# S5 set-up on VectorE, a new order of layer 0's input rows, and a norm shift subtracted last, in a two-layer encoder trunk

## The chip, the cores and the metric

The kernel runs on one core of a Trainium2 chip. The metric is the device time of one execution in microseconds (us), the median of the runs. TensorE (PE) multiplies matrices, and PEld is its loading of weights. VectorE (DVE), ScalarE (ACT) and GpSimd (POOL) work on elements, and SyncE (SP) issues the loads.

## What is computed

256 frames and 16 meta tokens (272 columns) of width 2048 pass through two layers, in float32. Each layer is a mixer and a SwiGLU feed-forward block, and each of them is wrapped in a residual and a norm, `x <- LayerNorm(alpha * x + f(x))`. Layer 0's mixer is one input projection whose 15 blocks of 128 rows go to two parts: rows 0 to 7 to S5, a complex diagonal state space (eight quarters q of 128 channels here), rows 8 to 14 to latent attention (8 to 11 the query latents, 12 and 13 the key and value latents, 14 the rotary key). For S5 the reference has:

```python
dt = jnp.exp(log_dt)[:, None]
mag = jnp.exp(dt * a_re)
ab_re = mag * jnp.cos(dt * a_im)
ab_im = mag * jnp.sin(dt * a_im)
...
bb_re = f_re[..., None] * b_re - f_im[..., None] * b_im
...
_, _, s_re, s_im = lax.associative_scan(...)   # s_t = ab * s_(t-1) + bb u_t, complex
y = (einsum('lbgp,gjp->blgj', s_re, c_re) - einsum('lbgp,gjp->blgj', s_im, c_im))
```

Layer 1's mixer is Mamba-2; it is not touched.

## The kernel before

**Matmuls.** `linear()` (L131) walks through a projection in the order of the table SEQ (L58), block by block of 128x128. `weights()` (L113) brings eight blocks at a time: SP loads a tile `st` of 128x1024 (four buffers), ACT casts it to `hi` (L126), DVE computes `lo = st - hi` (L127; three buffers each). Every block takes three matmuls: hi by the high part of the input (L173), hi by its low part (L174), lo by its high part (L175). A tile thus feeds 24 matmuls, and PE can go on only when ACT and DVE have done their parts. Accumulators `mm_...` have three PSUM buffers, which an evacuation frees.

**Order.** The program is written in plain loops, and a scheduler of the tile framework sorts each engine's instructions; then every engine runs its own in that order, and an instruction that waits holds up all behind it on its engine. The order at the places of the change is shown below for that reason.

**Layer 0's mixer** (L516). in0b is the first projection, rows 0, 1 and 8, all three together while the input is loaded and split (L536, L537: `xin`, `h`); then in0a, rows 9 to 14 one by one; then uq and ukv, which need the norms of the latents (`rms`, L561), the values, and the scores of 8 heads with rows 2 to 7 between them. `evac_u` (L591) receives rows 0 and 1: on row 0 it calls `S.load()`, loads the constants, and calls `S.setup()` and `S.run(0)`.

**S5** (L972). `load` brings the parameters `prm`. `setup` (L1034) computes on DVE the two exponentials (`expm1`), on ACT the sine and cosine, and then powers of the complex numbers with `cmul` (L985), six operations for one product, on POOL: `pr, pi` (powers of the step), `wr, wi` (repeated squares), and from them the tables `er, ei, gr, gi`. `prep(q)` (L1140) builds the matrices `gb` and `ca` of a quarter on POOL (`pp`), which ACT copies; `prep_pe(q)` (L1173) transposes gb on PE (`gt_p`), multiplies (`kb_p`), and makes the rotation tables `ec, es` on DVE from er, ei, gr, gi. `run(q)` (L1208) writes u to DRAM and loads it shifted (`u2`), multiplies (`w_p`), rotates and scans on DVE, and forms the output (`s5y_p`); then it prepares the next quarter.

**The norms.** `ln_add` (L303) adds a row of a projection's result to x as it comes out of PSUM (L311). The sums that the norm needs are taken of `x - k`, with k a shift that is known only after row 0 (`ln_sums`, L319, copied at L328); so each of the rows 1 to 15 has k subtracted first (L308), and its addends are added then. Four norms go this way: behind out0a, dn_b0, out1c and dn_b1.

## Time and profile before

| | |
|---|---|
| median of 3 runs | 2692.54 us (2691.0 to 2699.14) |
| the profiled execution | 2692.83 us, its span 2691.0 us |
| busy share of the span | PE 98%, PEld 92%, DVE 65%, ACT 49%, POOL 12% |
| DMA | 173 GB/s in the mean |
| granted TensorE clock, mean of the span | 0.99 of full speed (2.4 GHz); the other level is 0.50 (1.2 GHz) |

The page gives busy times over the whole execution; what an engine waited for, and when, is read from the lists of waits, from windows, and from the timelines of single engines. Times in them are us from the start of the span. Lines are those of the kernel before.

### The profile page before, as it was taken

What the parts mean: (1) busy time and instruction counts of PE and PEld (TensorE: products, weight loads), DVE (VectorE), ACT (ScalarE), POOL (GpSimd) and SP (SyncE); (2) the same over time, 40 slices, a digit from 0 to 9 for tenths busy, and PEclk for the clock granted to TensorE, in tenths of its full rate; (3) what the DMA queues carried; (4) which work ended last, traced back from release to release, by engine and by line L of the source; (5) the groups of instructions that cost most, each with busy time, mean ns of one, the idle gap of its engine ahead of it and who ended that gap; (6) DMA issues with size and microseconds to landing.
All of it is one profiled execution on the core that took longest, in us unless ns stands there. A gap on an engine that the chain in (4) does not pass through costs nothing.

```text
span 2691.0 us, 48314 instructions
## 1 busy us (share of the span) xinstructions
PE 2634.4 (98%) x19344; PEld 2468.3 (92%) x19344; DVE 1737.1 (65%) x2944; ACT 1316.6 (49%) x2168; POOL 331.2 (12%) x484
## 2 busy tenths in 40 slices
PE   9899999999999999999999999999999999999997
PEld 9677999999999999999999899999998888888886
DVE  7768678444444445669778875788975555555565
ACT  5545447334334334448656653554664443444443
POOL 5844040000000000210002110111300000000022
PEclk9898999999999999999999999999999999999998
DMA  7233544555555554545645555544555555555553
GB/s 246 85 111 90 194 151 166 177 173 175 178 173 175 177 173 165 184 165 173 220 156 195 176 175 186 177 168 149 181 196 188 188 188 187 187 188 188 183 189 116
DMA packets 139666, 465.01 MB, mean 173 GB/s; under 512 B 14832, under 2 KB 30000, under 8 KB 139312
## 3 DMA queue, kind: packets, MB, share of 16 engines
q1 hardware_dynamic: 139296, 461.71, 51.5%
q8 instruction: 151, 2.47, 0.4%
q14 instruction: 75, 0.61, 0.1%
q10 hardware_dynamic: 144, 0.21, 0.0%
HBM read 458.58 MB, written 3.28 MB: 172 GB/s over the span
## 4 chain that ended last, share of the span: by engine, by line
PE 88%; DVE 6%; POOL 3%; ACT 1%; issue 1%; DMA 0%; SPq 0%; DVEq 0%; ACTq 0%; POOLq 0%
PE mm_gu_b L170 6%; PE mm_gu_a L170 5%; PE mm_in L170 4%; PE mm_gu_a L175 4%; PE mm_gu_a L173 4%; PE mm_gu_a L174 4%; PE mm_gu_b L175 3%; PE mm_gu_b L173 3%; PE mm_gu_b L174 3%; PE mm_gu_b L171 3%; PE mm_dn_b L170 3%; PE mm_dn_a L170 3%; PE mm_in L174 2%; PE mm_gu_a L171 2%; PE mm_in L173 2%; PE mm_in L175 2%
## 5 line engine op out<-in xcount | busy, mean ns | idle before, releaser
L127 DVE TENSOR_TENSOR lo_gu_b<-st_gu_b,hi_gu_b 128x1024 fp32r<-128x1024 f32 x176 | 215.6, 1225 | 228.7 <-ACT hi_gu_b L126 228.7
L127 DVE TENSOR_TENSOR lo_gu_a<-st_gu_a,hi_gu_a 128x1024 fp32r<-128x1024 f32 x176 | 216.0, 1227 | 176.7 <-ACT hi_gu_a L126 176.1
L126 ACT CAST hi_gu_b<-st_gu_b 128x1024 fp32r<-128x1024 f32 x176 | 184.8, 1050 | 290.4 <-issue 155.7
L126 ACT CAST hi_gu_a<-st_gu_a 128x1024 fp32r<-128x1024 f32 x176 | 184.7, 1049 | 232.7 <-issue 121.1
L339 POOL TENSOR_TENSOR ln_s<-ln_s,ln_q 128x272 f32<-128x272 f32 (+1 forms) x58 | 71.9, 1239 | 1563.2 <-ACT ln_q L334 1562.8
L170 PE MATMUL mm_gu_b<-m,hi_gu_b 128*128 128x512 f32 x704 | 246.8, 395 | 0.0
L127 DVE TENSOR_TENSOR lo_in<-st_in,hi_in 128x512 fp32r<-128x512 f32 (+1 forms) x268 | 184.9, 723 | 82.1 <-ACT hi_in L126 78.3
L126 ACT CAST hi_in<-st_in 128x512 fp32r<-128x512 f32 (+1 forms) x268 | 158.4, 636 | 116.9 <-PE mm_in L174 38.1
L175 PE MATMUL mm_gu_a<-mix,lo_gu_a 128*128 128x272 f32 (+1 forms) x704 | 203.4, 289 | 1.7 <-DVE lo_gu_a L127 1.6
L174 PE MATMUL mm_gu_a<-mix,hi_gu_a 128*128 128x272 f32 (+1 forms) x704 | 203.5, 289 | 0.0
L175 PE MATMUL mm_gu_b<-mix,lo_gu_b 128*128 128x272 f32 x704 | 203.2, 289 | 0.0
L174 PE MATMUL mm_gu_b<-mix,hi_gu_b 128*128 128x272 f32 x704 | 202.7, 288 | 0.0
L173 PE MATMUL mm_gu_a<-mix,hi_gu_a 128*128 128x272 f32 (+1 forms) x704 | 202.5, 288 | 0.0
L173 PE MATMUL mm_gu_b<-mix,hi_gu_b 128*128 128x272 f32 x704 | 202.5, 288 | 0.0
L171 PE MATMUL mm_gu_b<-m,lo_gu_b 128*128 128x256 f32 x704 | 197.2, 280 | 0.0
L170 PE MATMUL mm_gu_a<-m,hi_gu_a 128*128 128x512 f32 x544 | 190.7, 395 | 0.0
L170 PE MATMUL mm_in<-f,hi_in 128*128 128x512 f32 x512 | 181.0, 396 | 0.0
L127 DVE TENSOR_TENSOR lo_dn_a<-st_dn_a,hi_dn_a 128x1024 fp32r<-128x1024 f32 x88 | 107.8, 1225 | 110.4 <-ACT hi_dn_a L126 110.0
L126 ACT CAST hi_dn_a<-st_dn_a 128x1024 fp32r<-128x1024 f32 x88 | 92.3, 1049 | 162.2 <-PE mm_dn_a L174 78.6
L170 PEld LDWEIGHTS mm_gu_b<-m,hi_gu_b 128*128 128x128 f32 x704 | 132.5, 188 | 31.2
L127 DVE TENSOR_TENSOR lo_dn_b<-st_dn_b,hi_dn_b 128x1024 fp32r<-128x1024 f32 x88 | 107.6, 1224 | 78.0 <-ACT hi_dn_b L126 77.6
L126 ACT CAST hi_dn_b<-st_dn_b 128x1024 fp32r<-128x1024 f32 x88 | 92.3, 1049 | 129.8 <-PE mm_dn_b L170 46.9
(549 smaller groups left out, 8630.0 us busy)
## 6 DMA issues: line engine op xcount, KB each, us to landing
st_gu_a<-in_w_gu_a SPq DMA_DIRECT2D x176, 512.0 KB, 3.9
st_gu_b<-in_w_gu_b SPq DMA_DIRECT2D x176, 512.0 KB, 4.2
st_in<-in_w_in SPq DMA_DIRECT2D x140, 512.0 KB, 3.4
st_dn_a<-in_w_dn_a SPq DMA_DIRECT2D x88, 512.0 KB, 4.2
st_dn_b<-in_w_dn_b SPq DMA_DIRECT2D x88, 512.0 KB, 3.8
st_in1h<-in_w_in1h SPq DMA_DIRECT2D x34, 512.0 KB, 3.3
st_out1a<-in_w_out1a SPq DMA_DIRECT2D x32, 512.0 KB, 3.3
st_out0b<-in_w_out0b SPq DMA_DIRECT2D x16, 512.0 KB, 3.5
```

Of the source, the lines that this page charges most:

```text
L126: nc.scalar.copy(hi[:, j:j + w], st[:, j:j + w])
L127: nc.vector.tensor_tensor(lo[:, j:j + w], st[:, j:j + w], hi[:, j:j + w], op=ALU.subtract)
L170: nc.tensor.matmul(ps[m].rearrange("p (a b) -> p a b", a=2), lhsT=wh, rhs=x2, start=st, stop=False)
L171: nc.tensor.matmul(o, lhsT=wl, rhs=xh, start=False, stop=left[m] == 0)
L173: nc.tensor.matmul(o, lhsT=wh, rhs=xh, start=st, stop=False)
L174: nc.tensor.matmul(o, lhsT=wh, rhs=xl, start=False, stop=False)
L175: nc.tensor.matmul(o, lhsT=wl, rhs=xh, start=False, stop=left[m] == 0)
L339: nc.gpsimd.tensor_tensor(st["s2"], st["s2"], q, op=ALU.add)
```

## The change

The complex numbers of S5's set-up are packed, real and imaginary part side by side in one tile (`z1`, `pw`, `wz`, `ez`, `gz`), and their 18 products go from POOL's `cmul` to DVE: ten squares in three instructions (`zsqr`) and eight products in four (`zmul`). POOL loses 108 instructions. in0b takes rows 8, 9 and 10, in0a rows 11 to 14 and then 0 and 1. `S.load()` comes first of all, the constants and `S.setup()` behind in0b; `S.run(0)` is called behind uq and `S.run(1)` behind the values, and the first `prep_pe(0)` and `prep(1)` move from the set-up into `run(0)`. In `ln_add` the subtraction of k comes behind the addends.

```diff
@@ -56,8 +56,8 @@
 
 
 SEQ = {
-    "in0a": seq_rows([9, 10, 11, 12, 13, 14], range(16)),
-    "in0b": seq_rows([0, 1, 8], range(16), 3),
+    "in0a": seq_rows([11, 12, 13, 14, 0, 1], range(16)),
+    "in0b": seq_rows([8, 9, 10], range(16), 3),
     "in0_2": seq_rows([2], range(16)),
     "in0_3": seq_rows([3], range(16)),
     "in0_4": seq_rows([4], range(16)),
@@ -304,11 +304,11 @@
 
         nc, pool, n, xs = self.nc, st["pool"], st["n"], st["xs"]
         x = xs[i]
-        if i:
-            nc.vector.tensor_tensor(x, x, st["k"], op=ALU.subtract)
         for a in (p, q):
             if a is not None:
                 nc.vector.tensor_tensor(x, x, a, op=ALU.add)
+        if i:
+            nc.vector.tensor_tensor(x, x, st["k"], op=ALU.subtract)
         self.ln_sums(st, i, x)
         if st["hx"] is not None:
             if i >= st["late"]:
@@ -589,20 +589,21 @@
             S = S5(self, s5, ps, u)
 
             def evac_u(m, p):
-                if m == 8:
+                nc.scalar.copy(u[:, m, :], p)
+                S.run(m)
+
+            def evac_0(m, p):
+                if m < 8:
+                    nc.scalar.copy(u[:, m, :], p)
+                else:
                     evac_a(m, p)
-                    return
-                nc.scalar.copy(u[:, m, :], p)
-                if m == 0:
-                    S.load()
-                    for t, a in ((self.ident, "ident"), (self.vecs, "vecs"), (cos, "cos"), (sin, "sin"),
-                                 (perm, "perm")):
-                        nc.sync.dma_start(t, A[a])
-                    S.setup()
-                S.run(m)
-
-            self.linear("in0b", rhs, evac_u, N)
-            self.linear("in0a", rhs, evac_a, N)
+
+            S.load()
+            self.linear("in0b", rhs, evac_0, N)
+            for t, a in ((self.ident, "ident"), (self.vecs, "vecs"), (cos, "cos"), (sin, "sin"), (perm, "perm")):
+                nc.sync.dma_start(t, A[a])
+            S.setup()
+            self.linear("in0a", rhs, evac_0, N)
 
             qk = self.res.tile([P, DT, N], F32, tag="x", name="qk")
             qr = pool.tile([P, 4, N], F32, tag="qr", name="qrope")
@@ -618,6 +619,7 @@
             def evac_k(m, p):
                 nc.scalar.copy(qk[:, 8 + m, :], p)
 
+            S.run(0)
             self.linear("ukv", lambda k, m: kn[:, :, k, :], evac_k, N)
 
 
@@ -640,6 +642,7 @@
             self.dump("kr", kr)
             self.dump("v", v)
 
+            S.run(1)
             probs = self.scores(pool, work, pa, 0, qk, qr, kr)
             for h in range(8):
                 nxt = self.scores(pool, work, pa, h + 1, qk, qr, kr) if h < 7 else None
@@ -1004,6 +1007,29 @@
         eng.tensor_tensor(t1, ai, br, op=ALU.mult)
         eng.tensor_tensor(oim, t3, t1, op=ALU.add)
 
+    def zmul(self, o, a, b, shape):
+
+        v = self.nc.vector
+        n = 2 * int(np.prod(shape))
+        t1, t2 = (self.t(f"zm{c}", [n], tag=f"cm{c}", bufs=1) for c in range(2))
+        if len(shape) == 2:
+            t1, t2 = (x.rearrange("p (r a b) -> p r a b", r=2, b=shape[1]) for x in (t1, t2))
+            br, bi = (b[:, c].unsqueeze(2).unsqueeze(1).to_broadcast([P, 2] + shape) for c in range(2))
+        else:
+            t1, t2 = (x.rearrange("p (r a) -> p r a", r=2) for x in (t1, t2))
+            br, bi = (b[:, c].unsqueeze(1).to_broadcast([P, 2] + shape) for c in range(2))
+        v.tensor_tensor(t1, a, br, op=ALU.mult)
+        v.tensor_tensor(t2, a, bi, op=ALU.mult)
+        v.tensor_tensor(o[:, 0], t1[:, 0], t2[:, 1], op=ALU.subtract)
+        v.tensor_tensor(o[:, 1], t1[:, 1], t2[:, 0], op=ALU.add)
+
+    def zsqr(self, o, a):
+        v = self.nc.vector
+        t = self.t("zs", [64], tag="cm2", bufs=1).rearrange("p (r a) -> p r a", r=2)
+        v.tensor_tensor(t, a, a, op=ALU.mult)
+        v.scalar_tensor_tensor(o[:, 1], a[:, 0], 2.0, a[:, 1], op0=ALU.mult, op1=ALU.mult)
+        v.tensor_tensor(o[:, 0], t[:, 0], t[:, 1], op=ALU.subtract)
+
     def expm1(self, x, name):
 
         v = self.nc.vector
@@ -1048,7 +1074,9 @@
         v.scalar_tensor_tensor(r, k, -1.9350051879882812e-3, r, op0=ALU.mult, op1=ALU.add)
         v.scalar_tensor_tensor(r, k, -3.0199159819e-7, r, op0=ALU.mult, op1=ALU.add)
         v.tensor_scalar(r, r, -3.1415925, 3.1415925, op0=ALU.max, op1=ALU.min)
-        sn, cs, hs, ab = (self.t(n_, [32], tag=t_) for n_, t_ in (("sn", "sn"), ("csn", "csn"), ("hs", "pp2"), ("ab", "ro3")))
+        z1 = self.t("z1", [2, 32])
+        cs, sn = z1[:, 0], z1[:, 1]
+        hs, ab = (self.t(n_, [32], tag=t_) for n_, t_ in (("hs", "pp2"), ("ab", "ro3")))
         nc.scalar.activation(ab, r, AF.Abs)
         nc.scalar.activation(sn, r, AF.Sin)
         nc.scalar.activation(cs, ab, AF.Sin, bias=T.halfpi, scale=-1.0)
@@ -1059,22 +1087,17 @@
         v.tensor_tensor(q2, cs, cs, op=ALU.mult)
         v.tensor_tensor(q, q, q2, op=ALU.add)
         v.tensor_scalar(q, q, -0.5, 1.5, op0=ALU.mult, op1=ALU.add)
-        v.tensor_tensor(sn, sn, q, op=ALU.mult)
-        v.tensor_tensor(cs, cs, q, op=ALU.mult)
-
-        pr, pi = self.t("pr", [32, 5]), self.t("pi", [32, 5])
+        v.tensor_tensor(z1, z1, q.unsqueeze(1).to_broadcast([P, 2, 32]), op=ALU.mult)
+
+        pw = self.t("pw", [2, 5, 32])
+        pr, pi = pw[:, 0].rearrange("p k s -> p s k"), pw[:, 1].rearrange("p k s -> p s k")
         self.pr, self.pi = pr, pi
-        nc.gpsimd.memset(pr[:, :, 4], 1.0)
-        nc.gpsimd.memset(pi[:, :, 4], 0.0)
-        v.tensor_tensor(pr[:, :, 3], mag, cs, op=ALU.mult)
-        v.tensor_tensor(pi[:, :, 3], mag, sn, op=ALU.mult)
-
-        def pw(o, a, b):
-            self.cmul(nc.gpsimd, pr[:, :, o], pi[:, :, o], pr[:, :, a], pi[:, :, a], pr[:, :, b], pi[:, :, b], [32])
-
-        pw(2, 3, 3)
-        pw(1, 2, 3)
-        pw(0, 2, 2)
+        nc.gpsimd.memset(pw[:, 0, 4], 1.0)
+        nc.gpsimd.memset(pw[:, 1, 4], 0.0)
+        v.tensor_tensor(pw[:, :, 3], z1, mag.unsqueeze(1).to_broadcast([P, 2, 32]), op=ALU.mult)
+        self.zsqr(pw[:, :, 2], pw[:, :, 3])
+        self.zmul(pw[:, :, 1], pw[:, :, 2], pw[:, :, 3], [32])
+        self.zsqr(pw[:, :, 0], pw[:, :, 2])
         self.m4 = self.t("m4", [32])
         v.tensor_tensor(q, mag, mag, op=ALU.mult)
         v.tensor_tensor(self.m4, q, q, op=ALU.mult)
@@ -1098,27 +1121,21 @@
         v.tensor_tensor(fi, fi, den, op=ALU.mult)
         self.fr, self.fi = fr, fi
 
-        er, ei = self.t("er", [32, 8]), self.t("ei", [32, 8])
-        gr, gi = self.t("gr", [32, 9]), self.t("gi", [32, 9])
-        wr, wi = self.t("wr", [32, 7], tag="pp0"), self.t("wi", [32, 7], tag="pp1")
-
-        def sqr(o, i):
-            self.cmul(nc.gpsimd, wr[:, :, o], wi[:, :, o], wr[:, :, i], wi[:, :, i], wr[:, :, i], wi[:, :, i], [32])
-
-
-        self.cmul(nc.gpsimd, wr[:, :, 1], wi[:, :, 1], cs, sn, cs, sn, [32])
-        self.cmul(nc.gpsimd, wr[:, :, 0], wi[:, :, 0], wr[:, :, 1], wi[:, :, 1], wr[:, :, 1], wi[:, :, 1], [32])
+        ez, gz = self.t("ez", [2, 32, 8]), self.t("gz", [2, 32, 9])
+        er, ei, gr, gi = ez[:, 0], ez[:, 1], gz[:, 0], gz[:, 1]
+
+        wz = self.t("wz", [2, 7, 32], tag="u2", bufs=1)
+        self.zsqr(wz[:, :, 1], z1)
+        self.zsqr(wz[:, :, 0], wz[:, :, 1])
         for j in range(1, 7):
-            sqr(j, j - 1)
-        for (tr, ti, lo, n) in ((er, ei, 0, 8), (gr, gi, 3, 9)):
-            nc.gpsimd.memset(tr[:, :, 0], 1.0)
-            nc.gpsimd.memset(ti[:, :, 0], 0.0)
+            self.zsqr(wz[:, :, j], wz[:, :, j - 1])
+        for (tz, lo, n) in ((ez, 0, 8), (gz, 3, 9)):
+            nc.gpsimd.memset(tz[:, 0, :, 0], 1.0)
+            nc.gpsimd.memset(tz[:, 1, :, 0], 0.0)
             w, j = 1, lo
             while w < n:
                 m = min(w, n - w)
-                br = wr[:, :, j:j + 1].to_broadcast([P, 32, m])
-                bi = wi[:, :, j:j + 1].to_broadcast([P, 32, m])
-                self.cmul(nc.gpsimd, tr[:, :, w:w + m], ti[:, :, w:w + m], tr[:, :, 0:m], ti[:, :, 0:m], br, bi, [32, m])
+                self.zmul(tz[:, :, :, w:w + m], tz[:, :, :, 0:m], wz[:, :, j], [32, m])
                 w, j = 2 * w, j + 1
         self.er, self.ei, self.gr, self.gi = er, ei, gr, gi
 
@@ -1134,8 +1151,6 @@
             self.zb.append((gb, ca, kb, m4))
         self.ready = {}
         self.prep(0)
-        self.prep_pe(0)
-        self.prep(1)
 
     def prep(self, q):
 
@@ -1208,6 +1223,9 @@
     def run(self, q):
         nc, T, u = self.nc, self.T, self.u
         v = nc.vector
+        if q == 0:
+            self.prep_pe(0)
+            self.prep(1)
         gb, ca, kb, m4 = self.zb[q % 2]
         gt, ec, es = self.ready.pop(q)
```

The order of the instructions, at three places. **DVE at the start of the program**, before (`h` is the low part of the input, `lo_in0b` the low part of a weight tile):

```order
L127 TENSOR_TENSOR lo_in0b_107<-st_in0b_104,hi_in0b_106 128x1024
L208 TENSOR_TENSOR h_82<-xin,h_82 128x2x272 x2
L127 TENSOR_TENSOR lo_in0b_147<-st_in0b_144,hi_in0b_146 128x1024
L208 TENSOR_TENSOR h_82<-xin,h_82 128x2x272
L127 TENSOR_TENSOR lo_in0b_180<-st_in0b_177,hi_in0b_179 128x1024
L208 TENSOR_TENSOR h_82<-xin,h_82 128x2x272
L127 TENSOR_TENSOR lo_in0b_213<-st_in0b_210,hi_in0b_212 128x1024
```

and with the change:

```order
L1039 TENSOR_SCALAR ex_328<-prm 128x32
L1040 TENSOR_SCALAR ex_323<-prm 128x32
L1110 TENSOR_TENSOR den<-prm 128x32
L1041 TENSOR_SCALAR ex_324<-ex_323 128x32
L1042 TENSOR_SCALAR ex_324<-ex_324 128x32
L1043 SCALAR_TENSOR_TENSOR ex_325<-ex_324,ex_323 128x32
L1049 TENSOR_SCALAR ex_i<-ex_324 128x32
L1044 SCALAR_TENSOR_TENSOR ex_325<-ex_324,ex_325 128x32
L1050 TENSOR_TENSOR ex_327<-ex_i,ex_328 128x32
L1045 TENSOR_SCALAR ex_326<-ex_325 128x32
L1047 SCALAR_TENSOR_TENSOR ex_326<-ex_326,ex_325 128x32 x5
L127 TENSOR_TENSOR lo_in0b_109<-st_in0b_106,hi_in0b_108 128x1024
```

Fifteen operations on the S5 parameters (`prm`, `ex`) now stand ahead of the first weight tile.

**PE in uq, around the transposes gt_p of quarter 0**, before:

```order
L173 MATMUL mm_uq_1642<-qn,hi_uq_1624 128x272
L174 MATMUL mm_uq_1642<-qn,hi_uq_1624 128x272
L175 MATMUL mm_uq_1642<-qn,lo_uq_1625 128x272
L1183 MATMUL gt_p<-ident,gb 128x128 x8
L173 MATMUL mm_uq_1662<-qn,hi_uq_1658 128x272
L174 MATMUL mm_uq_1662<-qn,hi_uq_1658 128x272
```

and with the change, where these rows come 75 places earlier on PE:

```order
L174 MATMUL mm_uq_1066<-qn,hi_uq_1048 128x272
L175 MATMUL mm_uq_1066<-qn,lo_uq_1049 128x272
L1198 MATMUL gt_p<-ident,gb 128x128 x5
L234 MATMUL spread<-diag,ones 128x272
L555 MATMUL rope_sw<-rope_x,perm 128x272
L173 MATMUL mm_uq_1086<-qn,hi_uq_1082 128x272
L174 MATMUL mm_uq_1086<-qn,hi_uq_1082 128x272
```

The eight transposes stood in one block near the end of uq; now five stand after uq's first tile, and the others follow between its later matmuls.

**DVE in out0a, at the first rows of the norm** (`ln_k` is the shift k, L329 its subtraction from row 0), before:

```order
L208 TENSOR_TENSOR mix<-sg,mix 128x272
L311 TENSOR_TENSOR x_3475<-x_3475,mm_out0a_4319 128x272
L127 TENSOR_TENSOR lo_out0a_4430<-st_out0a_4427,hi_out0a_4429 128x1024
L127 TENSOR_TENSOR lo_out0a_4467<-st_out0a_4464,hi_out0a_4466 128x1024
L127 TENSOR_TENSOR lo_out0a_4504<-st_out0a_4501,hi_out0a_4503 128x1024
L329 TENSOR_TENSOR x_3475<-x_3475,ln_k 128x272
L308 TENSOR_TENSOR x_3475<-x_3475,ln_k 128x272 x14
L311 TENSOR_TENSOR x_3475<-x_3475,mm_out0a_4359 128x272
L311 TENSOR_TENSOR x_3475<-x_3475,mm_out0a_4396 128x272
L311 TENSOR_TENSOR x_3475<-x_3475,mm_out0a_4433 128x272
```

and with the change (L309 is the addition, L311 the subtraction now):

```order
L208 TENSOR_TENSOR mix<-sg,mix 128x272
L309 TENSOR_TENSOR x_3394<-x_3394,mm_out0a_4238 128x272
L309 TENSOR_TENSOR x_3394<-x_3394,mm_out0a_4278 128x272
L127 TENSOR_TENSOR lo_out0a_4349<-st_out0a_4346,hi_out0a_4348 128x1024
L309 TENSOR_TENSOR x_3394<-x_3394,mm_out0a_4315 128x272
L127 TENSOR_TENSOR lo_out0a_4386<-st_out0a_4383,hi_out0a_4385 128x1024
L127 TENSOR_TENSOR lo_out0a_4423<-st_out0a_4420,hi_out0a_4422 128x1024
L329 TENSOR_TENSOR x_3394<-x_3394,ln_k 128x272
L311 TENSOR_TENSOR x_3394<-x_3394,ln_k 128x272 x2
L309 TENSOR_TENSOR x_3394<-x_3394,mm_out0a_4352 128x272
L338 TENSOR_TENSOR ln_s_4267<-x_3394 128x272
L311 TENSOR_TENSOR x_3394<-x_3394,ln_k 128x272
```

The fourteen subtractions in one block ahead of the additions of the rows 1 to 3 are gone; each row's subtraction follows its own addition, and weight tiles stand between them.

## Rows read from the trace of the kernel before

**Rows 1.** The page's first part: busy time, share of the span and instructions of each engine.

```profile
PE 2634.4 (98%) x19344; PEld 2468.3 (92%) x19344; DVE 1737.1 (65%) x2944; ACT 1316.6 (49%) x2168; POOL 331.2 (12%) x484
```

**Rows 2.** What TensorE waited for, whole run: its tile and line, the engine and line that ended the wait; us in all, times, the longest.

```profile
PE gt_p L1183 <- POOL cm L1004: 9.9, 1, 9.9
PE mm_in0b L173 <- ACT h L207: 5.7, 1, 5.7
PE mm_out0a L173 <- DVE x L311: 4.8, 1, 4.8
...
PE w_p L1223 <- ACT kb L1195: 2.3, 1, 2.3
PE s5y_p L1253 <- DVE mx L725: 2.1, 1, 2.1
PE s5y_p L1257 <- DVE vr L1247: 1.9, 2, 1.6
```

**Rows 3.** Four stretches: most of in0b; in0a; the gap ahead of gt_p; out1c. Columns: window, its length, then busy us (and instructions) of PE, PEld, DVE, ACT, POOL, the granted TensorE clock, the share of the DMA engines, GB/s.

```profile
5.70:26.40 20.70, 20.40 (x145) 20.08 (x146) 17.17 (x40) 11.91 (x16) 0.45 (x2) 1.00 0.97 349
26.40:63.50 37.10, 37.10 (x300) 37.02 (x299) 29.15 (x87) 20.97 (x36) 27.64 (x66) 1.00 0.65 203
...
76.90:86.80 9.90, 0.35 (x3) 0.12 (x1) 0.27 (x1) 0.52 (x2) 9.34 (x27) 0.76 0.00 0
1876.00:1920.00 44.00, 41.00 (x332) 39.46 (x330) 43.65 (x77) 26.66 (x57) 20.75 (x19) 1.00 0.47 156
```

**Rows 4.** POOL's timeline, 33 to 95 us: start, length, line, operation, tiles, in brackets the idle time ahead of it and what ended it. L1001 and L1005 are lines of cmul, L1164 and L1163 of prep.

```profile
33.75 1.33 POOL L1001 TENSOR_TENSOR cm<-pi 128x32 f32<-128x32 f32 x1 [27.59 <-DVE pi L1070]
35.04 0.24 POOL L1000 TENSOR_TENSOR cm<-pr 128x32 f32<-128x32 f32 x1
...
84.22 0.26 POOL L1005 TENSOR_TENSOR gi<-cm,cm 128x32 f32<-128x32 f32 x1
...
85.00 0.29 POOL L1000 TENSOR_TENSOR cm<-bc,fr 128x64 f32<-128x64 f32 x1
...
85.50 0.72 POOL L1164 TENSOR_TENSOR pp<-pp,pp 128x256 f32<-128x256 f32 x1
...
89.16 0.94 POOL L1163 TENSOR_TENSOR pp<-pi,ci 128x320 f32<-128x320 f32 x1
```

**Rows 5.** DVE's timeline, 86 to 95 us (the ec and es of prep_pe(0), and two weight tiles); columns as in 4.

```profile
86.53 0.46 DVE L1001 TENSOR_TENSOR cm<-gi,ei 128x288 f32<-128x288 f32 x1 [11.53 <-POOL cr L1003]
86.91 0.53 DVE L208 TENSOR_TENSOR kn<-kvl,kn 128x272 fp32r<-128x272 f32 x1
...
89.43 0.98 DVE L1002 TENSOR_TENSOR cm<-gr,ei 128x288 f32<-128x288 f32 x1
...
94.09 1.65 DVE L127 TENSOR_TENSOR lo_ukv<-st_ukv,hi_ukv 128x1024 fp32r<-128x1024 f32 x1
```

**Rows 6.** Stretches of 4 us behind the gap, behind w_p, and in out0a; columns as in 3.

```profile
84.00:88.00 4.00, 0.81 (x4) 0.84 (x5) 1.47 (x3) 1.69 (x3) 3.92 (x11) 0.50 0.00 0
88.00:92.00 4.00, 4.00 (x20) 3.91 (x19) 3.79 (x4) 3.40 (x9) 4.00 (x6) 0.50 0.14 35
100.00:104.00 4.00, 2.33 (x11) 2.10 (x12) 3.47 (x7) 3.59 (x11) 4.00 (x8) 0.81 0.39 142
104.00:108.00 4.00, 4.00 (x23) 3.76 (x23) 4.00 (x6) 2.11 (x5) 4.00 (x4) 0.76 0.53 137
348.00:352.00 4.00, 1.01 (x4) 1.04 (x5) 4.00 (x12) 1.12 (x3) 0.56 (x1) 0.53 0.28 111
352.00:356.00 4.00, 4.00 (x23) 4.00 (x22) 1.38 (x3) 0.01 (x1) 3.84 (x4) 0.61 0.38 130
```

**Rows 7.** DVE's timeline in out0a, 345 to 351 us; columns as in 4.

```profile
345.13 0.43 DVE L329 TENSOR_TENSOR x<-x,ln_k 128x272 f32<-128x272 f32 x1
345.49 5.01 DVE L308 TENSOR_TENSOR x<-x,ln_k 128x272 f32<-128x272 f32 x14
350.42 1.12 DVE L311 TENSOR_TENSOR x<-x,mm_out0a 128x272 f32<-128x272 f32 x3
```

**Rows 8.** DVE's timeline in in0a, 28 to 30 us: a weight tile and small set-up operations; columns as in 4.

```profile
28.02 1.23 DVE L127 TENSOR_TENSOR lo_in0a<-st_in0a,hi_in0a 128x1024 fp32r<-128x1024 f32 x1
29.16 0.18 DVE L1048 SCALAR_TENSOR_TENSOR r<-k,r 128x32 f32<-128x32 f32 x1
29.26 0.18 DVE L1021 SCALAR_TENSOR_TENSOR ex<-ex,ex 128x32 f32<-128x32 f32 x1
...
29.71 0.42 DVE L1021 SCALAR_TENSOR_TENSOR ex<-ex,ex 128x32 f32<-128x32 f32 x2
```

**Rows 9.** DVE's groups by line and shape in in0a, 26.4 to 63.5 us: count, busy us, mean ns of one, idle time ahead of them and what ended it.

```profile
L127 DVE TENSOR_TENSOR lo_in0a<-st_in0a,hi_in0a 128x1024 fp32r<-128x1024 f32 x11 | 13.7, 1256 | 4.5 <-ACT hi_in0a L126 4.4
```

**Rows 10.** SP's queue at the start: the issue of the first weight tile; columns as in 4.

```profile
0.74 0.38 SPq L121 DMA_DIRECT2D st_in0b<-in_w_in0b  x1
```

**Rows 11.** DVE's timeline at the start: its first operation; columns as in 4.

```profile
5.12 1.23 DVE L127 TENSOR_TENSOR lo_in0b<-st_in0b,hi_in0b 128x1024 fp32r<-128x1024 f32 x1 [5.12 <-ACT hi_in0b L126]
```

**Rows 12.** DMA issues of the first 20 us: tile, engine, count, KB each, median us to landing.

```profile
prm<-in_s5p SPq DMA_DIRECT2D x1, 48.0 KB, 6.4
```

**Rows 13.** DVE's timeline in dn_b0 (the norm's subtractions) and at the end of the kernel (the last additions of dn_b1); columns as in 4.

```profile
1070.29 5.01 DVE L308 TENSOR_TENSOR x<-x,ln_k 128x272 f32<-128x272 f32 x14
...
2669.95 0.88 DVE L311 TENSOR_TENSOR x<-x,mm_dn_b 128x256 f32<-128x256 f32 x2 [7.21 <-PE mm_dn_b L171]
```

## The prediction

> **What bounds the kernel now.** I read the page's first part, then the list of what TensorE (PE) waited for, then windows of the stretches where it waited. PE is busy 98% of the span and VectorE (DVE) 65% [rows 1], so a microsecond counts only where PE stands still, runs at its lower clock, or has not begun. The list of waits [rows 2] is short, and its top names what this change touches: 9.9 us in which gt_p, the transposes of the S5 matrices, waits for GpSimd (POOL), and 4.8 us in which out0a's second group of matmuls waits for DVE at L311. The wait of 5.7 us for `h` is the start of the kernel.
>
> The first wait stands in the windows by stage [rows 3]: in in0b and in0a PE is never idle, in the 9.9 us from 76.9 it does 0.35 us of work and POOL 9.34. POOL began its chain of small operations at 33.75, when DVE had made `pi`, and ended the set-up at 84.2 [rows 4]; one 128x32 operation took 0.24 us when free and 1.33 beside a DVE subtraction of a weight tile. DVE stood behind the same chain for 11.5 us [rows 5]. After the gap PE was granted its lower level (0.50 of 2.4 GHz is 1.2 GHz) until about 92 us [rows 6]. The second wait is plain in DVE's own row [rows 7]: fourteen subtractions of the norm's shift, 5.01 us, stand in one block ahead of the first addition that would free a PSUM buffer.
>
> **The change part by part.**
>
> *The POOL chain goes.* 108 of POOL's operations leave its queue; what remains there is the preparation of one head's gb and ca (prep), which now needs only the packed powers that DVE makes in about 15 rows after the sine. gt_p then has its operands some 20 us before it is reached: prep(0) can begin near 31 us, needs at most 11.7 us of free POOL time (six operations of 128x256 at 0.72, six of 128x320 at 0.94, six of 128x64 at 0.29 [rows 4]), and gt_p stands behind 459 matmuls, of which 445 were done at 63.5 [rows 3]: about 66 us. I take the whole wait, **-9.9**. The clock after it: 0.81 us busy at 0.50 in 84 to 88 and 4.00 us at 0.50 in 88 to 92 [rows 6]; half of 4.8 us, **-2.4**, comes back too, because PE is not idle ahead of it. Bounds for both: 0 (another wait takes the place) to -12.3.
>
> *S5 of head 0 starts ahead of uq's end.* kb_p comes some 50 matmuls before w_p(0); before, it stood directly ahead of it. w_p's wait of 2.3 us for kb [rows 2] and the lower clock behind it (0.81 and 0.76 in 100 to 108 [rows 6], 0.24 of 4.00 us and 0.19 of 2.33, 1.4 us) could both go: 0 to -3.7. S5's other waits of 1 to 2 us [rows 2] may come back in another place, so I take half, **-1.9**.
>
> *DVE takes 60 more instructions, and others earlier.* zsqr and zmul are 62 instructions: 28 of 128x32, 22 of 128x64, 8 of 128x128, 4 of 128x256. A 128x32 operation follows the last one in 0.10 us (29.16 to 29.26) or in 0.21 where it needs its result, [rows 8]; a 128x288 one took 0.38 to its successor at 86.53 [rows 5]. A straight line from 0.11 to 0.38 gives 28x0.11 + 22x0.145 + 8x0.21 + 4x0.35 = 9.4 us; packing saves two, 0.2. Six 128x288 operations of ec and es come ahead of the last in0a subtraction, 6x0.38 = 2.3; one of the two uq subtractions that lay in that stretch before does not, -1.2. What the order moves from in0a into in0b cancels when both stages are taken together: DVE 17.17 + 29.15 = 46.3 us busy of 57.8 [rows 3], then 46.3 + 9.2 + 2.3 - 1.2 = 56.6. The cover is therefore nearly used up: PE waits for a `lo` tile of 1.23 us [rows 8] about every 3 us, and DVE has 1.2 us in hand over 19 tiles. On top come collisions with POOL's prep, which lies in the same stretch. The nearest rows on both sides: beside 66 POOL operations the eleven subtractions of in0a had a mean of 1.256 us [rows 9], against 1.23 free [rows 8], so nearly nothing; beside prep's larger ones a 128x288 operation took 0.98 and a weight tile 1.65 [rows 5]. About 20 collisions at 0 to 0.5 us are 0 to 10. I take **+3**, nearer the first row, since a weight tile meets at most some ten of prep's operations.
>
> *The start.* prm is loaded first, one issue of 0.38 us on SP's queue ahead of the first weight tile [rows 10], and DVE has fifteen operations on prm (about 2.9 us at 0.10 to 0.21 each) ahead of the first lo, which it did at 5.12 [rows 11]. If prm lands about 2.5 us after its issue, lo comes at 5.5 to 6; its landing of 6.4 us before [rows 12] was behind other transfers, and would make it 10. Bounds 0.4 to 5, taken **+0.8**, since the queue is empty.
>
> *The norms.* At out0a the first additions no longer stand behind the block of subtractions; PSUM buffers come free when their sums end, so the 4.8 us go [rows 2, 7], **-4.8**. The lower clock behind it goes too: 1.01 us at 0.53 in 348 to 352 and 4.00 us at 0.61 in 352 to 356 [rows 6]: 0.47x1.01 + 0.39x4.00 = **-2.0**. DVE's total does not change, it is only spread out, and the lo tiles follow within it. In dn_b0 the same block of 5.01 us delays no matmul in the list of waits [rows 2, 13], so nothing; in out1c DVE is busy 43.65 of 44 us and PE 41.0 [rows 3]: DVE is the bound there, and a new order of the same work moves it by no more than about 1 us either way, 0. Behind the last addend a norm now ends one subtraction later, 0.36 us (5.01 / 14); at the kernel's end that lies on the path, since the last additions are what the end waits for [rows 13], at two of the other three norms perhaps half of it: **+0.7**.
>
> Sum: -9.9 - 2.4 - 1.9 + 3 + 0.8 - 4.8 - 2.0 + 0.7 = -16.5. The profiled execution took 2692.83, which is the median of the runs (2692.54) to 0.3 us: **2676.3**.
>
> **Rivals.** *A: DVE and POOL shut each other out.* If each of prep(0)'s operations holds DVE up for its whole length, the two stages need 56.6 + 11.7 = 68.3 of 57.8, a stall of 10.5 in place of 3: 2683.8. For it: the 0.98 and 1.65 us above [rows 5], and the POOL operation that took 1.33 us in place of 0.24 [rows 4]. Against: there POOL waited, not DVE, and the mean of 1.256 [rows 9]. Chance 0.13. The Trainium skill (SBUF — State Buffer, "Who interferes with whom") states that a VectorE instruction with two SBUF inputs contends with a GpSimd instruction that reads SBUF, and that whichever comes second blocks in full. The rows agree that something blocks; by that rule the stall would be this rival's, and it speaks against putting more work on DVE beside prep.
>
> *B, slower than before: DVE becomes the bound of the first two stages.* The same collisions, but on DVE's many small steps, in a queue without slack, and with prep(1) in the same stretch. It turns the gain into a loss when DVE's 56.6 us stretch by more than (57.8 + 3 + 16.5) / 56.6 = 1.37; at 1.5 the stall is 27.1 us: 2700.4. For it: tile subtractions at 1.65 are 1.35 times as long, the 128x288 ones over twice [rows 5]. Against: POOL would have to run through the whole stretch, and it has 108 operations fewer. Chance 0.05.
>
> *C: the S5 work of heads 0 and 1 is later overall and comes back as waits.* Its chain (u to DRAM and back, w_p, the scans, s5y_p) now starts at the end of in0a, and head 0 and 1 lie among the scores. Each of its waits measured 1.9 to 2.3 us [rows 2]; three of them are 6: 2682.3. Chance 0.16.
>
> *D: out0a's wait is replaced.* If the additions are held by something else there (the lo tiles behind them on DVE, which is busy 4.00 of 4 us [rows 6]), the 6.8 us stay: 2683.1. Chance 0.09.
>
> *E: the change does not do what it says: gt_p still waits*, now for prep(0) behind the load of bc, or for ACT's copies of gb that sit in ACT's queue ahead of the casts. The 12.3 us stay: 2688.6. Chance 0.07.
>
> **How the numbers follow.** The forecast has the remaining 0.50. About 0.3% (8.1 us) is what a measurement can tell from no change, so faster means under 2684.5. The forecast counts as faster with 0.49, C with 0.12, A with 0.08, D with 0.06 and E with 0.02: 0.77. Within 0.3%: the rest of these, and 0.01 of B: 0.18. Slower: 0.05, about all of B. The low end takes no stall on DVE (-3), the w_p term whole (-1.8), the start at its bound (-0.4) and 4 us from S5's other waits: 2667. The high end is E's, 2689; B and the worst of A lie outside.
>
> **What would show it.** In the profile after: no gt_p wait for POOL, and PE busy through 60 to 100 us at full clock; POOL with about 110 instructions fewer; DVE over 95% busy from 10 to 60 us, and waits of PE for lo_in0a or lo_uq of 0 to 6 us in all; at out0a no block of fourteen subtractions and no wait over 1 us; PE's first matmul within 1 us of 5.7. Wrong would be: waits for lo tiles of over 10 us (A, B), new S5 waits above 5 us (C), or a new wait under gt_p's name (E).

## The result and the profile after

The changed kernel takes 2671.76 us (median of 4 runs, 2669.08 to 2672.41), before 2692.48: a ratio of 0.9918, 95% interval 0.9906 to 0.993. Five runs more on another chip gave 2671.92 and 0.9914 (0.9902 to 0.9927). The forecast was 2676.3 in 2667 to 2689. The profiled execution took 2672.05, its span is 2670.3.

The page's first part, against [rows 1]; columns as there:

```profile
PE 2626.6 (98%) x19344; PEld 2461.5 (92%) x19344; DVE 1747.2 (65%) x3004; ACT 1317.6 (49%) x2170; POOL 295.9 (11%) x376
```

DVE has 60 instructions more, POOL 108 fewer. What PE waited for, against [rows 2]:

```profile
PE mm_in0b L173 <- ACT h L207: 6.9, 1, 6.9
PE spread L234 <- DVE diag L230: 2.1, 1, 2.1
PE w_p L1241 <- DVE mx L729: 2.0, 1, 2.0
PE w_p L1241 <- ACT kb L1210: 1.9, 2, 1.6
PE mm_in0a L175 <- DVE lo_in0a L127: 1.7, 1, 1.7
...
PE mm_uq L175 <- DVE lo_uq L127: 1.3, 1, 1.3
```

gt_p's wait of 9.9 us and out0a's of 4.8 have left the list. New are `spread`, `mm_in0a` and `mm_uq`, all for DVE and all between 64 and 80 us (`diag` and `spread` bring the factor of the latents' norm to all partitions). Windows after (columns as in [rows 3]): four of 4 us in that stretch, two long ones behind it, and the place in out0a where the block of subtractions was:

```profile
64.00:68.00 4.00, 2.27 (x18) 2.05 (x17) 3.37 (x7) 2.32 (x5) 4.00 (x4) 1.00 0.19 66
68.00:72.00 4.00, 2.66 (x21) 2.44 (x20) 3.02 (x5) 0.22 (x2) 4.00 (x8) 1.00 0.42 135
72.00:76.00 4.00, 2.51 (x21) 2.27 (x19) 3.83 (x10) 4.00 (x8) 1.41 (x2) 1.00 0.77 214
76.00:80.00 4.00, 3.38 (x23) 3.25 (x24) 3.96 (x8) 1.02 (x4) 0.00 (x0) 1.00 0.99 268
84.00:144.00 60.00, 60.00 (x497) 44.30 (x495) 42.82 (x97) 37.19 (x90) 32.98 (x42) 1.00 0.34 106
144.00:200.00 56.00, 56.00 (x522) 48.18 (x521) 43.41 (x121) 28.77 (x81) 32.15 (x37) 1.00 0.40 118
326.00:342.00 16.00, 16.00 (x128) 15.92 (x127) 11.84 (x19) 8.22 (x12) 5.72 (x5) 1.00 0.49 157
```

In the four windows PE is idle for 5.2 us in all. From 84 to 200 us it is never idle and never at the lower clock, and not in the window in out0a either. What that is worth is seen in two windows of the kernel before, behind its gap:

```profile
104.00:144.00 40.00, 37.39 (x321) 24.58 (x321) 36.68 (x87) 22.08 (x57) 29.64 (x36) 0.97 0.27 87
144.00:200.00 56.00, 55.10 (x509) 46.75 (x500) 36.46 (x92) 28.27 (x77) 26.95 (x36) 0.97 0.37 109
```

There 3.5 us were idle, and a clock of 0.97 over 92.5 us busy cost 2.8 more: 6.3 us, and now none.

Where the time went is read off the starts of PE's matmuls, by tile (us from the start of the span; first or last start of a stage):

| | in0b last | in0a last | values last | out0b first | out0a first | out0a last | out1c first | out1c last | span |
|---|---|---|---|---|---|---|---|---|---|
| before | 26.2 | 63.4 | 138.5 | 254.8 | 333.5 | 388.9 | 1869.0 | 1918.4 | 2691.0 |
| changed | 29.3 | 69.0 | 128.6 | 242.6 | 322.0 | 370.5 | 1850.1 | 1896.6 | 2670.3 |
| e1, set-up and order alone | 29.0 | 69.5 | 129.0 | 244.6 | 324.3 | 379.4 | 1859.3 | 1908.3 | 2680.9 |
| e2, norm alone | 26.8 | 64.0 | 139.1 | 253.2 | 332.0 | 380.5 | 1860.0 | 1906.5 | 2680.4 |
| e3, set-up on POOL | 28.8 | 67.9 | 134.7 | 259.3 | 338.4 | 387.0 | 1865.0 | 1911.4 | 2686.4 |
| e4, order as before | 27.1 | 65.7 | 145.5 | 252.0 | 331.4 | 380.0 | 1858.0 | 1904.4 | 2678.1 |
| e6, prm loaded later | 26.0 | 63.8 | 121.4 | 241.0 | 320.7 | 369.2 | 1847.3 | 1893.8 | 2668.4 |
| e10, that and nci on POOL | 26.8 | 64.5 | 124.2 | 238.6 | 319.4 | 367.9 | 1846.0 | 1892.4 | 2666.9 |
| e11, products twice | 29.1 | 66.9 | 129.2 | 245.9 | 325.0 | 373.6 | 1851.6 | 1898.0 | 2672.6 |

The changed kernel is 5.6 us behind at the end of in0a, 12.2 ahead when out0b begins, 18.4 ahead at out0a's end and 21.8 at out1c's. Out0a alone went from 55.4 to 48.5 us, out1c from 49.4 to 46.5.

### The profile page after: what moved, and what is told of

It reads as the page before. It is cut to its first block, busy times and chain, and to the rows that moved or that the text cites. A ratio compares the mean times of both kernels' runs of the same rounds, so it can differ in the third digit from the quotient of the medians.

```text
span 2670.3 us, 48252 instructions
## 1 busy us (share of the span) xinstructions
PE 2626.6 (98%) x19344; PEld 2461.5 (92%) x19344; DVE 1747.2 (65%) x3004; ACT 1317.6 (49%) x2170; POOL 295.9 (11%) x376
## 4 chain that ended last, share of the span: by engine, by line
PE 87%; DVE 7%; POOL 2%; issue 2%; ACT 1%; DMA 0%; DVEq 0%; ACTq 0%; POOLq 0%
PE mm_gu_b L170 6%; PE mm_gu_a L170 5%; PE mm_in L170 4%; PE mm_gu_a L175 4%; PE mm_gu_a L174 4%; PE mm_gu_a L173 4%; PE mm_gu_b L175 3%; PE mm_gu_b L173 3%; PE mm_gu_b L174 3%; PE mm_gu_b L171 3%; PE mm_dn_b L170 3%; PE mm_dn_a L170 3%; PE mm_in L174 2%; PE mm_in L175 2%; PE mm_gu_a L171 2%; PE mm_in L173 2%
```

## The experiments

All ratios are to the kernel before, run beside each on the same chip. The order of all instructions is found anew for every kernel, so an edit in one place shifts others; differences of 1 or 2 us are read with that in mind.

**The two parts apart.** e1 puts the subtraction back ahead of the addends in the changed kernel; e2 makes that one edit in the kernel before:

```diff
-        if i:
-            nc.vector.tensor_tensor(x, x, st["k"], op=ALU.subtract)
         for a in (p, q):
...
+        if i:
+            nc.vector.tensor_tensor(x, x, st["k"], op=ALU.subtract)
```

> The set-up on VectorE and the new order of rows, with the norm's subtraction of the shift ahead of the addends as before. Theory (the change is a sum of two parts that do not touch each other): out0a's block of fourteen subtractions is back with its wait of 4.8 us and the lower clock behind it (6.8 us), and some 3 us at out1c, where out1c ended 2.9 us further ahead than it began: 2681 to 2683, and the traces agree with the changed kernel up to out0a. Rival (the norm's new order gained nothing in itself, out0a only came at a better time): 2671 to 2674. Rival (the two parts help each other, as out0a's buffers are met in another state): 2684 to 2688.

> The kernel before with the norm's subtraction behind the addends, and nothing else. Theory: 6.8 us at out0a and about 3 at out1c come, 0.35 go at the end of the kernel: 2682.5 to 2684, with gt_p's wait of 9.9 us still there. Rival (nothing at out1c): 2685.5 to 2687. Rival (the part helps only together with the other): 2690 to 2693.

e1: 2681.79, ratio 0.9948 (0.9934 to 0.9961). e2: 2682.59, 0.9956 (0.9942 to 0.997). Both lie in the ranges of their theories. Of 2692.5 the ratios are 14.0 and 11.8 us, together 25.8, where both parts made 22.1 and, on the second chip, 23.2; each ratio is uncertain by about 3.5 us, so the sum is confirmed no closer than that. (The kernel before measured 2695.18 beside e1 and e2, so the differences of the medians to 2692.5 would be too small.) The stages say more: out0a is 55.1 us long in e1 and 48.5 in e2, out1c 49.0 and 46.5. So the gain in both places is the norm's, and nothing shows that the parts help each other. e1's out0b begins 2.0 us later than the changed kernel's although its edit lies behind that place: the waits ahead of it are the same, but the clock granted from 226 to 242 us was 0.59 there and 0.72 in the changed kernel. Two traces of the same work differ by that much.

**The set-up's engine, and the order.** e3 takes `setup` from before (`cmul` on POOL) into the changed kernel; e4 keeps zsqr and zmul and takes SEQ, `evac_u`, the load of prm and the calls of the S5 steps from before ("the order" below is all of these).

```diff
-            self.zsqr(wz[:, :, j], wz[:, :, j - 1])            # e3
+            sqr(j, j - 1)
-    "in0b": seq_rows([8, 9, 10], range(16), 3),                # e4
+    "in0b": seq_rows([0, 1, 8], range(16), 3),
```

> The changed kernel with the set-up's 18 complex products back on GpSimd, in six instructions each; order of rows, places of S.run, and norm as changed. Theory (the length of GpSimd's chain made the wait): the chain is 50 us long and begins only some 6 us sooner, so gt_p still waits for GpSimd, 4 to 12 us, while VectorE's waits of 5 us in in0a and uq shrink: 2673 to 2682. Rival (the new order of rows alone gives gt_p time enough): no wait for GpSimd above 1 us, and 2666 to 2671, faster than the changed kernel, since VectorE has less to do.

> The changed kernel with the order of rows, the load of prm and the calls of the S5 steps as before; set-up on VectorE and the norm as changed. Theory (the set-up's engine is what counts): gt_p's wait is gone, the start is back at the old one (2 us sooner: the first tile's lo at 5.1 and not 7.1 us), and VectorE is less full in in0b: 2668 to 2675. Rival (both are needed: without the new order the set-up lies so late on VectorE that gt_p or w_p wait): a wait of 5 us or more at gt_p, kb_p or w_p, 2677 to 2684.

e3: 2683.17 (2679.59 to 2688.18), 0.9954 (0.994 to 0.9968). e4: 2679.84, 0.994 (0.9928 to 0.9953). What PE waited for, e3:

```profile
PE gt_p L1207 <- POOL cm L1007: 10.3, 1, 10.3
```

and e4:

```profile
PE w_p L1237 <- ACT kb L1209: 6.4, 1, 6.4
...
PE kb_p L1204 <- POOL pp L1181: 4.5, 1, 4.5
PE mm_uq L173 <- ACT qk L612: 4.5, 1, 4.5
```

In e3 the wait of gt_p is back at 10.3 us, as the theory had it, though its time lies 1 us above the range. In e4 gt_p waits no more, but w_p, kb_p and uq wait 15.4 us, so the theory fell and the rival held. All of them have the norm's new order, so e2 (2682.59) is what to compare with: the set-up alone gains 2.8 us, the order alone nothing clear of noise (-0.6), both together (the changed kernel, on other chips) 10.8: neither does it by itself. (In the table out0b begins 2.8 us earlier, 4.5 later and 12.2 earlier than before; e3's profiled execution took 2688.18, 5.0 us above its median, so the 4.5 are not the price of the order.) With the set-up on DVE the chain is short; only with the new order does it also lie early enough.

**The late start, and the stall at 64 to 80 us.** DVE's first operations in the changed kernel (start, length, line, operation):

```profile
2.66 0.96 DVE L1039 TENSOR_SCALAR ex<-prm 128x32 f32<-128x32 f32 x1 [2.66 <-DMA prm<-in_s5p]
...
4.47 0.19 DVE L1043 SCALAR_TENSOR_TENSOR ex<-ex,ex 128x32 f32<-128x32 f32 x1
4.58 1.00 DVE L1049 TENSOR_SCALAR ex_i<-ex 128x32 int32<-128x32 f32 x1
...
7.12 1.22 DVE L127 TENSOR_TENSOR lo_in0b<-st_in0b,hi_in0b 128x1024 fp32r<-128x1024 f32 x1
```

and what POOL did meanwhile:

```profile
2.42 1.17 POOL L1150 MEMSET ca<- 128x1280 f32 x1
...
4.35 1.19 POOL L1150 MEMSET ca<- 128x1280 f32 x1
```

prm landed by 2.66 us, no later than the forecast took it, but operations of 0.17 to 0.19 us lasted 0.96 and 1.00, each to just where a memset of 128x1280 on POOL ended (2.42 + 1.17, 4.35 + 1.19). The first lo came at 7.12 and not 5.12. The Trainium skill (SBUF — State Buffer, "Who interferes with whom") says that a VectorE instruction with at most one SBUF input is free of GpSimd unless it runs in one of the 2-port modes, which it lists as open to tensor_scalar. The rows agree with that: the six TENSOR_SCALAR operations ahead of the first lo each ended within 0.06 us of the end of a memset, and what was queued right behind them ended with them, while the SCALAR_TENSOR_TENSOR at 4.47, beside the memset of 4.35, took its 0.19. Which mode they ran in the rows do not show.

In the later stretch three queues hold each other. POOL (prep of quarters 0 and 1):

```profile
48.81 1.70 POOL L1005 TENSOR_TENSOR cm<-bc,fi 128x64 f32<-128x64 f32 x1 [12.46 <-DVE wz L1031]
52.40 0.48 POOL L1003 TENSOR_TENSOR cm<-bc,fr 128x64 f32<-128x64 f32 x1 [1.90 <-DVE rs_r L257]
...
65.05 2.82 POOL L1181 TENSOR_TENSOR pp<-pw,bc 128x256 f32<-128x256 f32 x1
...
71.43 0.32 POOL L1008 TENSOR_TENSOR ci<-cm,cm 128x64 f32<-128x64 f32 x1
```

DVE:

```profile
57.25 0.46 DVE L1003 TENSOR_TENSOR cm<-gz,ez 128x288 f32<-128x288 f32 x1 [1.91 <-POOL ci L1008]
57.63 1.02 DVE L1005 TENSOR_TENSOR cm<-gz,ez 128x288 f32<-128x288 f32 x1
...
65.03 1.21 DVE L127 TENSOR_TENSOR lo_in0a<-st_in0a,hi_in0a 128x1024 fp32r<-128x1024 f32 x1
...
68.69 0.89 DVE L1004 TENSOR_TENSOR cm<-gz,ez 128x288 f32<-128x288 f32 x1 [1.32 <-POOL cr L1006]
```

ScalarE:

```profile
57.25 0.26 ACT L1167 ACTIVATE nci<-ci 128x64 f32<-128x64 f32 x1 [1.74 <-POOL ci L1008]
...
62.07 1.05 ACT L126 CAST hi_in0a<-st_in0a 128x1024 fp32r<-128x1024 f32 x1
...
71.78 0.26 ACT L1167 ACTIVATE nci<-ci 128x64 f32<-128x64 f32 x1 [5.26 <-POOL ci L1008]
```

POOL waits 12.5 us for the squares on DVE, since both use the scratch tiles of `cmul`; one operation of 128x256 then lasts 2.82 us beside DVE's work. DVE's ec and es wait 1.9 and 1.3 us for POOL, and ScalarE's negation `nci` 1.7 and 5.3; the casts `hi` stand behind it. Seven kernels tried the links, cut here to the lines that matter (e5 and e7 put the products into the buffer of `gt` and the squares into one of their own; e9 and e10 move `nci` in all eight quarters, e12 in the first two only):

```diff
-        t1, t2 = (self.t(f"zm{c}", [n], tag=f"cm{c}", bufs=1) for c in range(2))      # e5, e7: other buffers
+        zm = self.t("zm", [1024], tag="gt", bufs=1)
-            S.load()                                                                  # e6, e7, e10
             self.linear("in0b", rhs, evac_0, N)
+            S.load()
-        nc.scalar.mul(nci, ci, -1.0)                                                  # e9, e10
+        g.tensor_scalar(nci, ci, -1.0, None, op0=ALU.mult)
-                nc.scalar.copy(o[hs, 0, :, :, h, :], t1[hs])                          # e12: gb, ca, nci, q < 2
+                    g.tensor_copy(o[hs, 0, :, :, h, :], t1[hs])
+        if not again:                                                                 # e11, zsqr alike
+            self.zmul(o, a, b, shape, True)
```

> The changed kernel once more, as the measure for the three kernels beside it: 2670 to 2673.

> The changed kernel, with scratch tiles of their own for the squares and products on VectorE (no longer those of cmul, which prep on GpSimd and ec, es use). Theory (the 5.2 us in which PE stands still from 64 to 80 us come from the shared scratch: GpSimd's prep waits 12.5 us for VectorE's squares, and VectorE, 1.9 and 1.3 us, and ScalarE's casts, 1.7 to 5.3 us, then wait for GpSimd): GpSimd's prep(0) runs on without that wait, and 3 to 5 us come: 2667 to 2669. Rival 1 (VectorE is simply full there): 2671 to 2673, and PE waits for lo tiles as before. Rival 2 (the collisions of GpSimd and VectorE cost it, whenever prep runs): 2670 to 2674, with VectorE's operations of two inputs long beside prep in an earlier stretch.

> The changed kernel with the load of prm behind in0b's, so that no S5 operation stands ahead of the first weight tiles on VectorE. Theory (fifteen operations on prm, drawn out by GpSimd's memsets, put off the first lo tile by 2.0 us and the end of in0b by 3.1): the first lo at 5.1 to 5.3 us, in0b ends 2 to 3 us sooner, 2668.5 to 2670. Rival (S5's chain is later then, and the wait comes back in in0a, uq or at w_p): 2671 to 2676.

> Own scratch and the later load together. Theory (two separate losses): 2665 to 2667, the sum of both. Rival (the later chain meets a fuller VectorE in in0a, and takes back what the start gives): 2667 to 2670, no better than own scratch alone.

> The changed kernel, with the small negation of ci in prep on GpSimd and not on ScalarE, where it stood ahead of casts and waited 7.3 us for GpSimd. Theory (ScalarE's queue, held by that wait, puts off the casts of in0a and uq, and with them VectorE and PE): PE's idle time from 64 to 80 us shrinks by 2 to 4 of its 5.4 us: 2668 to 2670.5. Rival (VectorE has no slack there, and the casts would only wait for it): 2671 to 2673, the same waits for lo tiles. What is left of it under both: the copies of ca on ScalarE still wait for GpSimd.

> The negation on GpSimd together with the later load of prm (2669.7 without the negation). Theory as before: waits of 3 us at kb_p, lo_uq and qk from 68 to 80 us shrink, 2667 to 2669. Rival (the later chain is bounded by GpSimd's prep itself): 2669 to 2671.

> The changed kernel with every square and product of the set-up done twice on VectorE, 62 more instructions, 9.4 us by the prediction's own prices. Theory 1 (VectorE is full from 10 to 60 us): all of it reaches PE, 2679 to 2682, with waits for lo_in0a. Theory 2 (it has slack of some us, and what PE waited for is ScalarE behind GpSimd): 2673 to 2677.

> The changed kernel, with ScalarE's whole part in prep of quarters 0 and 1 (the negation and the copies of gb and ca) done on GpSimd, so that nothing in ScalarE's queue in in0a and uq waits for GpSimd. Theory (ScalarE's casts, held behind these, starve VectorE and PE from 64 to 80 us): no wait of ScalarE for GpSimd is left there, PE's idle time in that stretch falls from 5.2 us to under 2, and 2668 to 2670 unless gt_p or kb_p wait for GpSimd's longer queue. Rival (what holds PE is GpSimd's prep itself, through VectorE's ec and es, which wait for the shared scratch, and through its collisions): still 4 us or more idle from 64 to 80 us, or a new wait for GpSimd at gt_p, kb_p or w_p, and 2672 to 2678.

| | median us | ratio (95%) |
|---|---|---|
| the changed kernel again | 2671.92 | 0.9914 (0.9902 to 0.9927) |
| e5, own scratch | 2674.84 | 0.992 (0.9908 to 0.9932) |
| e6, prm loaded later | 2669.67 | 0.9903 (0.989 to 0.9916) |
| e7, both | 2672.93 | 0.9915 (0.9903 to 0.9928) |
| e9, nci on POOL | 2675.36 | 0.9928 (0.9915 to 0.9941) |
| e10, e6 with nci on POOL | 2668.05 | 0.99 (0.9886 to 0.9913) |
| e11, products twice | 2675.91 | 0.9933 (0.9919 to 0.9947) |
| e12, prep off ScalarE | 2671.31 | 0.9914 (0.9898 to 0.9929) |

*e6* held. DVE's first operation there:

```profile
5.39 1.23 DVE L127 TENSOR_TENSOR lo_in0b<-st_in0b,hi_in0b 128x1024 fp32r<-128x1024 f32 x1 [5.39 <-ACT hi_in0b L126]
```

in0b ends 3.3 us sooner, of which 1.6 are left when out0b begins and about 2 in the medians, both from one chip.

*e5* fell: POOL no longer waits for the squares, but prep now meets them. POOL, then ScalarE in e5:

```profile
42.09 2.11 POOL L1006 TENSOR_TENSOR cr<-cm,cm 128x64 f32<-128x64 f32 x1
...
46.38 0.32 POOL L1008 TENSOR_TENSOR ci<-cm,cm 128x64 f32<-128x64 f32 x1
...
58.49 3.90 POOL L1180 TENSOR_TENSOR pp<-pp,pp 128x256 f32<-128x256 f32 x1
```

```profile
38.84 1.04 ACT L126 CAST hi_in0a<-st_in0a 128x1024 fp32r<-128x1024 f32 x1
46.73 0.26 ACT L1168 ACTIVATE nci<-ci 128x64 f32<-128x64 f32 x1 [6.85 <-POOL ci L1008]
46.90 1.04 ACT L126 CAST hi_in0a<-st_in0a 128x1024 fp32r<-128x1024 f32 x1
```

An operation of 128x64, 0.3 us when free, takes 2.11, one of 128x256 takes 3.90; `nci` waits 6.85 us for `ci`, and in0a ends at 73.2 us. The stall moved into in0a and did not shrink: PE is idle for 3.9 us from 10 to 64 us, at a mean clock of 0.97, and for 0.5 from there to 80. *e7* fell with it: it is 3.3 us above e6, so the own scratch takes back what the later load gives, and its time lies above its rival's range too.

*e11* speaks against a DVE that is simply full. Its windows:

```profile
28.00:64.00 36.00, 36.00 (x294) 35.87 (x294) 35.52 (x145) 19.11 (x33) 5.45 (x6) 1.00 0.57 178
64.00:84.00 20.00, 20.00 (x158) 19.67 (x156) 18.00 (x55) 10.77 (x19) 10.65 (x12) 1.00 0.68 203
84.00:104.00 20.00, 16.36 (x100) 14.53 (x100) 19.58 (x28) 11.45 (x30) 17.44 (x23) 0.83 0.42 115
```

With 62 instructions more, DVE is 35.5 of 36 us busy in in0a, and PE is not idle at all up to 84 us, since prep falls later there. 3.6 us idle and the lower clock come behind it, 84 to 104, and 2.7 us idle from 104 to 144. The whole kernel loses 4 of the 9.4 us, as theory 2 had it.

*e9 and e12* tried ScalarE's part. e9's median is 3.4 us above the changed kernel's, with intervals that overlap; ScalarE still waits 6.3 us for POOL, at the copy of ca. From 64 to 80 us PE is idle for 4.1 us, at a mean clock of 0.81, so the theory's gain did not come. Its longest new wait lies far behind that stretch, at 233 us (0.9 in the changed kernel), so the whole time does not speak for this one link:

```profile
PE s5y_p L1271 <- DVE mx L728: 4.1, 1, 4.1
```

In e12 ScalarE waits for POOL nowhere from 28 to 100 us, and yet PE, in two of its windows:

```profile
64.00:68.00 4.00, 1.97 (x16) 1.75 (x15) 4.00 (x12) 3.40 (x7) 3.86 (x4) 1.00 0.06 10
68.00:72.00 4.00, 4.00 (x22) 4.00 (x21) 3.79 (x10) 1.07 (x2) 3.92 (x7) 0.57 0.91 283
```

is idle 2.0 us and then at 0.57 of the clock. From 64 to 80 us it is idle for 2.5 us and the lower clock costs 1.5, and 1.2 us idle lie just ahead and behind: in all as much as the 5.2 of the changed kernel. What is left is a wait of DVE (name of tile, line, releaser, us in all, times, longest):

```profile
DVE cm L1003 <- POOL ci L1008: 3.8, 2, 1.9
```

So taking ScalarE out changes nothing in the sum. The theory that its queue alone starves PE fell, and so did its rival's size. The runs fit one reading: prep of the first quarters, placed beside DVE's work in in0a and uq, holds PE through several links at once, and no link that was taken out alone brought a gain. For it speaks e11, where prep falls later and the stall with it. But no run takes prep out of that stretch and changes nothing else, so the reading is argued and not shown, and which links would have to go together is open. e10 has the lowest median (2666.1 to 2668.7, each run below every run of the changed kernel). Its 1.6 us below e6 are not put down to `nci`: on its chip the kernel before was 1.6 us faster too (2693.57 against 2695.13), and the two ratios do not tell them apart.

## Why the prediction was right, and where it was not

The mechanism was right: a chain of small operations on POOL, and one block of subtractions on DVE. The working did not ask whether the shorter chain or the earlier place takes the first wait away; e3 and e4 show that it takes both. The terms one by one:

- **gt_p, its clock, and w_p** (-14.2 forecast). The wait is gone, and with it everything behind it up to 200 us: 12.2 us idle and 3.0 of clock from 64 to 104, by windows of 4 us, and the 6.3 above: -21.5. With the new stall (5.2) and the start (3.1) that makes -13.2, of which 12.2 show when out0b begins. gt_p's 9.9 and the clock behind it came as forecast. The w_p term was mis-sized: I took half of 3.7 us and all of it went. Some 5 us more stood in no term; of the 3.5 idle behind 104 us 1.9 were ahead of `sc_a` (its line is below, at out1c) and 0.9 ahead of `att_o`, matmuls of the attention's heads, with a clock of 0.97 around them. Why these went is not shown.
- **DVE's new work** (+3). PE is idle 5.2 us, within the bounds but in another place and for another reason than a DVE without slack, so the size is luck. From 10 to 60 us DVE is busy for 45.9 of 50 us and PE for all 50, and e11 puts twice the products there without a wait of PE before 84 us. The working counted DVE's time and not the waits between three queues; the scratch tiles that zsqr shares with `cmul` were not looked at.
- **The start** (+0.8, bounds 0.4 to 5). 2.0 us at the first lo, 3.1 at the end of in0b: inside the bounds, above the value. The landing was as taken; POOL's memsets were overlooked.
- **out0a** (-6.8): 6.9. **The kernel's end** and the other norms (+0.7): the span lost 0.5 us between the last matmul and the end.
- **out1c** (0, at most about 1 either way): -2.9. This step failed. It took DVE's 43.65 us of 44 [rows 3] as a bound. But in the changed kernel DVE is as full behind the first rows (8.00 of 8 us), and PE does not wait: before, DVE's time went to fourteen subtractions that nothing waited for yet, ahead of an addition that frees a buffer. The wait stood in the list before, just below the lines of [rows 2]:

```profile
PE sc_a L713 <- ACT prob L727: 1.9, 1, 1.9
PE mm_out1c L173 <- DVE x L311: 1.5, 1, 1.5
```

The kernel before, by parts:

```profile
1869.00:1876.00 7.00, 7.00 (x62) 7.00 (x61) 3.58 (x9) 2.37 (x6) 0.00 (x0) 1.00 0.41 144
...
1884.00:1892.00 8.00, 6.75 (x57) 6.79 (x58) 8.00 (x16) 4.95 (x12) 4.46 (x5) 1.00 0.26 82
```

and the changed one:

```profile
1850.00:1857.00 7.00, 7.00 (x61) 7.00 (x60) 3.70 (x10) 2.31 (x6) 0.00 (x0) 1.00 0.44 146
1857.00:1865.00 8.00, 8.00 (x69) 7.95 (x68) 7.83 (x18) 5.90 (x14) 1.60 (x1) 1.00 0.52 178
1865.00:1873.00 8.00, 8.00 (x71) 8.00 (x70) 8.00 (x14) 5.37 (x12) 5.15 (x6) 1.00 0.42 126
1850.00:1897.00 47.00, 46.44 (x391) 46.01 (x389) 43.49 (x82) 28.20 (x62) 18.91 (x19) 1.00 0.51 167
```

Ahead of the block DVE was busy for about half of 7 us in both (3.58 and 3.70); then PE lost 1.25 us of 8 behind the block's start, and none of 16 now. The same work, begun when its addend comes, hides: PE is busy for 46.44 of 47 us.

The forecast lay 4.5 us above the measured time, but its misses were larger and partly cancelled: 7.3 us too little at gt_p and behind it and 2.9 at out1c, against a stall and a start that cost 2.2 and 2.3 more than taken. So it is in part luck that the sum came so near.

Rival E is refuted: no gt_p wait for POOL. D too, by e2. B as well: the weight tiles in in0a stay at 1.21 us. In A's place the rows show mostly the reverse: POOL is the one that is held up. C did not come: S5's waits before 200 us are gone, and those behind it add up to 5.7 us, against 5.9 before.

Of the signs named, four came: no gt_p wait, 108 instructions fewer, 3.0 us of waits for `lo` tiles in in0a and uq, out0a without a wait over 1 us. DVE was busy for 92% from 10 to 60 us, not over 95; PE was not busy through 60 to 100 us (5.2 idle), and its first matmul came 1.2 us late, not within 1.

## What to carry to other kernels

A wait for a chain can need two things together to go, as here a shorter chain and an earlier place; test them apart before crediting one. Look for work that stands in one block ahead of what frees a buffer, and put each piece behind its own input. An engine that is busy all through a window is not yet the bound: ask which of its work something waits for. Where a step is moved to another engine, look at the scratch tiles and the queues it shares, not at its durations alone; here freeing one of these at a time gained nothing.
